# Making the low part of every fourth weight block with an accumulating transfer instead of VectorE

## The chip, the cores and the metric

The kernel runs on one core of one Trainium2 chip. The metric is the device time of one execution in microseconds (us). The kernel before was run three times: 849.24 us median, 848.19 to 850.91.

A core has four compute engines that run at the same time and wait for each other with semaphores: TensorE (PE) multiplies matrices into PSUM, VectorE (DVE) does elementwise work with one or two inputs, ScalarE (ACT) applies a function to one input, GpSimd (POOL) does elementwise work and issues transfers of its own. SyncE (SP) issues transfers only. Sixteen DMA engines carry all transfers.

## The reference

Two layers of a decoder trunk on 256 tokens of width 1024. The stream is normalised and goes through one wide input projection; its columns feed three token mixers (a state-space scan, sliding-window attention with sinks, and forgetting attention), each with a SiLU gate. Each mixer's result is projected back to 1024 columns, the three are merged with sigmoid gates computed from the input, and one output projection is added to the stream:

```python
for layer in range(DEPTH):
    h = rms_norm(x, norm_w[layer])
    proj = jnp.einsum('bsd,de->bse', h, w_in[layer])
    ...
    branch = jnp.einsum('bsiw,iwd->bsid', ys, w_proj[layer])
    g = jax.nn.sigmoid(gates.reshape(b, s, N_BRANCH, d) + gate_bias[layer])
    merged = jnp.sum(g * branch, axis=2)
    x = x + jnp.einsum('bsd,de->bse', merged, w_out[layer])
return rms_norm(x, final_norm_w)
```

All in float32. Nearly all arithmetic is in the products with `w_in` (1024 x 12832), `w_proj` (three of 1024 x 1024) and `w_out` (1024 x 1024).

## The kernel before

**Split products.** TensorE is fed the type fp32r, to which a float32 number is rounded, and the kernel keeps accuracy by splitting both factors: a weight w is hi + lo, hi being w rounded to fp32r and lo the remainder w - hi, and the same for the activations. A product is three matmuls for each 128 rows of the contraction: high with high, low activation with high weight, high activation with low weight (`dense`, L278). So a unit asks for the hi of a weight first, and for the lo two matmuls later.

**Weight parts.** The weights come in pieces of 256 or 512 columns. A piece is cut along the contraction into parts of 128 x 1024 numbers (512 KB): two parts for 256 columns, four for 512. `stream` lists all parts of both layers in the order of use, 266 entries; two of them are narrow pieces of 32 columns that go another way. For a part `load_to` (L332) issues the load into a `raw` buffer on SP's queue (L341), `new_part` (L346) takes a `hi` and a `lo` buffer, and `split` (L261) fills them: ScalarE copies raw to hi (L264), VectorE subtracts hi from raw into lo (L265). There are six buffers each of raw, hi and lo. A part's raw is free again when its lo has been made, and only then can SP load the part six places later; SP's queue is in order. A part's hi and lo are free when PE has used them for the last time.

**How far ahead.** `feed` (L363) emits splits while fewer than AHEAD = 4 parts are held, and whenever PE's program needs a part that isn't there yet. `release` (L377) counts a part off when the last unit that uses it is through with it. A piece is used twice, by a unit for each half of the tokens or of the columns: first pass over all its parts, then a second pass, in which the parts are released one by one. `limit` (L372) stops the splits before the output projection and emits the next few with their place fixed (`pin`, shown as L259), so that they don't get in the way of the merge; that holds for parts 127 to 130 and 260 to 263.

**Order of the work.** PE's order is written out by hand: a list of units (`ops`), between which `pump` puts the small matmuls of the mixers (attention, scan, norms) as generators with delays in estimated PE time. The order of VectorE, ScalarE and GpSimd is made by the language's scheduler, except in the start phase and for pinned instructions. GpSimd does little: the sums of the rotary embedding (L492, L513), the causal selects on the bias of the forgetting attention (L867), powers for the norms (L226, L808) and one add of the merge (L936). Its only transfer is the rotary table at the start (L190).

**The stages.** A layer goes from keys and queries of the sliding window (pieces of 256 and 512) through its gates, convolution inputs, values and the first gate and projection pieces, then the forgetting attention's keys, queries and gates (256 each), then two runs of 512-wide gate and projection pieces (about 318 to 404 us in the first layer and 731 to 817 us in the second), then the output projection.

Of the kernel before, what the change touches and what calls it, by code (L numbers as in the profile page):

```python
# [11 lines left out]
F32 = mybir.dt.float32  # L12
F32R = mybir.dt.float32r
AF = mybir.ActivationFunctionType
ALU = mybir.AluOpType
# [13 lines left out]
T_PP, T_SSD, T_BIAS = 1, 1, 1  # L29
N_RAW, N_SPLIT = 6, 6  # L30
AHEAD = 4
WARM = 30
VERBOSE = False

# [9 lines left out]
def hybrid_trunk(  # L44
# [5 lines left out]
    nc = tc.nc  # L50
# [11 lines left out]
    def T(tag, shape, dtype=F32, bufs=None):  # L62
        count[0] += 1
        return sb.tile(shape, dtype, tag=tag, name=f"{tag}_{count[0]}",
                       bufs=bufs if bufs is not None else BUFS.get(tag, 1))
# [8 lines left out]
    def pmx():  # L74
        return PS("mx", 5)

    act = nc.scalar.activation
# [20 lines left out]
    def transpose(o, a, i):  # L98
        clock["t"] += 0.109
        nc.tensor.transpose(o, a, i)  # L100
# [160 lines left out]
    def split(hi, lo, src, scale=None, keep=lambda f: f):  # L261

        if scale is None:
            keep(act)(hi, src, AF.Copy)  # L264
            keep(tt)(lo, src, hi.bitcast(F32), op=ALU.subtract)  # L265
        else:
            keep(act)(hi, src, AF.Copy, scale=scale)
            keep(stt)(lo, src, scale, hi.bitcast(F32), op0=ALU.mult, op1=ALU.subtract)
# [46 lines left out]
    subs = []  # L315
    ops = []
    stream = []
    state = {"load": 0, "split": 0, "held": 0, "limit": None, "pin": False}
# [13 lines left out]
    def load_to(j):  # L332

        while state["load"] < min(j, len(stream)):
            i, k = stream[state["load"]]
            src, n = subs[i]
            kper = min(NK, 1024 // n)
            raw = T("raw" if n > 32 else "L1", [P, kper, n])
            for c, ap in src:
                m = ap.shape[-1]  # L340
                nc.sync.dma_start(raw[:, :, c:c + m],  # L341
                                  ap.rearrange("(k p) c -> p k c", p=P)[:, k:k + kper, :])
            raws[state["load"]] = raw
            state["load"] += 1

    def new_part():  # L346

        j = state["split"]
        i, _ = stream[j]
        n = subs[i][1]  # L350
        w = pieces.setdefault(i, Piece(n))
        load_to(j + 1)
        if n == 32:
            w.both = T("L2", [P, NK, 2 * n], F32R)
            hi, lo = w.both[:, :, 0:n], w.both[:, :, n:2 * n]
        else:
            hi, lo = T("hi", [P, w.kper, n], F32R), T("lo", [P, w.kper, n], F32R)
            state["held"] += 1
        w.parts.append((hi, lo))
        state["split"] += 1  # L360
        return raws.pop(j), hi, lo

    def feed(i=-1):  # L363

        lim = state["limit"]
        while state["split"] < len(stream) and state["split"] != lim and (
                state["held"] < AHEAD or stream[state["split"]][0] <= i):
            raw, hi, lo = new_part()
            split(hi, lo, raw, keep=pin if state["pin"] else lambda f: f)
            load_to(state["split"] + N_RAW)  # L370

    def limit(j, keep):  # L372

        state["limit"], state["pin"] = j, keep
        feed()

    def release(w, n):  # L377
        if w.n > 32 and n > w.released:
            state["held"] -= n - w.released
            w.released = n  # L380
            feed()

    def run_op(i, f, last):
        if i is None:
            f()
            return
        feed(i)
        w = pieces[i]
        w.last = last
        f(w)  # L390
        if last:
            release(w, NK // w.kper)
# [746 lines left out]
    with tc.manual_schedule(engines={ENG.PE, ENG.DVE, ENG.Activation, ENG.Pool}):  # L1139
        load_to(N_RAW)  # L1140
        warm = pmx()
        for i in range(WARM):
            transpose(warm[:, 0:P], ident, ident)
# [78 lines left out]
```

## Time and profile before

| | before |
|---|---|
| median of three runs | 849.24 us (848.19 to 850.91) |
| the profiled execution: span | 846.0 us (its time outside the span isn't recorded) |
| PE busy | 833.7 us, 99% |
| VectorE busy | 642.3 us, 76% |
| ScalarE busy | 511.6 us, 60% |
| GpSimd busy | 105.7 us, 12% |
| HBM read | 155.22 MB, 186 GB/s over the span |
| TensorE clock granted | 0.996 |

The span runs from the first instruction to the last. "L265 DVE lo<-raw,hi" is a group of instructions: line, engine, what it writes and reads by the program's names, then shapes, count, busy time in us, mean ns of one, and the engine's idle time just before with what ended it. "PEld" is TensorE's weight load, "SPq" the sequencer that issues transfers. Matmuls are pipelined, so a PE row's duration overlaps its neighbours; the distance of their starts is what one costs.

### The profile page before, as it was taken

The page shows a single profiled execution, that of the slowest core. Times are in us where ns is not written, and L with a number is a line of the kernel's source. Part 1 is how long each engine was busy: PE and PEld are TensorE (multiplying, and loading weights), DVE is VectorE, ACT ScalarE, POOL GpSimd, SP SyncE. Part 2 cuts the span into 40 slices and gives each one's busy share as a digit, 9 for nine tenths or more (in the row PEclk, how much of TensorE's full clock was granted, in tenths as well). Part 3 has the DMA queues.
Part 4 walks back from the last instruction along what each step waited for, and adds up shares of the span by engine and source line. Part 5 has one row for each costly group of instructions (what it writes and reads, how often), then busy time and mean ns, then how long its engine had stood idle before and what let it go on. Part 6 is the DMA issues. An engine that isn't in the chain of part 4 may idle for free.

```text
span 846.0 us, 15985 instructions
## 1 busy us (share of the span) xinstructions
PE 833.7 (99%) x5964; PEld 763.4 (90%) x5964; DVE 642.3 (76%) x1403; ACT 511.6 (60%) x1004; POOL 105.7 (12%) x134
## 2 busy tenths in 40 slices
PE   8999999999999999999999999999999999999996
PEld 7989898998999998888989998899899999988896
DVE  5777997998776669656788879879968567785665
ACT  6466777665666667435555667776557667654442
POOL 6410100000140010210014001000003110121000
PEclk9999999999999999999999999999999999999999
DMA  9576565666465545748676465465755654576632
GB/s 303 160 226 197 180 199 163 197 212 184 143 188 177 181 145 189 230 147 292 206 237 218 144 204 157 145 200 182 239 172 176 174 175 152 161 236 211 212 100 76
DMA packets 126638, 158.43 MB, mean 187 GB/s; under 512 B 12784, under 2 KB 88224, under 8 KB 126560
## 3 DMA queue, kind: packets, MB, share of 16 engines
q1 hardware_dynamic: 109456, 140.79, 52.5%
q10 hardware_dynamic: 17056, 16.49, 6.3%
q8 instruction: 47, 0.77, 0.4%
q14 instruction: 31, 0.25, 0.1%
q0 software_dynamic: 48, 0.13, 0.0%
HBM read 155.22 MB, written 2.16 MB: 186 GB/s over the span
## 4 chain that ended last, share of the span: by engine, by line
PE 95%; DMA 3%; DVE 1%; ACT 0%; POOL 0%; issue 0%; SPq 0%; POOLq 0%; DVEq 0%
PE mm L96 82%; PE mx L96 9%; PE mx L100 4%; DMA raw<-in_w_in_dram 3%; DVE lo L265 0%; POOL lo L1154 0%; ACT hi L1153 0%; DVE L L470 0%; ACT L L1013 0%; DVE L L265 0%; ACT L L264 0%; POOLq L1218 0%; ACT L L215 0%; DVE L L996 0%; DVE L L1001 0%
## 5 line engine op out<-in xcount | busy, mean ns | idle before, releaser
L265 DVE TENSOR_TENSOR lo<-raw,hi 128x1024 fp32r<-128x1024 f32 x252 | 308.3, 1235 | 93.8 <-ACT hi L264 84.6
L96 PE MATMUL mm<-hi,L 128*128 128x512 f32 (+1 forms) x1344 | 373.9, 364 | 2.0 <-ACT hi L1153 1.5
L264 ACT ACTIVATE hi<-raw 128x1024 fp32r<-128x1024 f32 x252 | 263.4, 1056 | 93.5 <-PE mm L96 75.5
L96 PE MATMUL mm<-L,hi 128*128 128x256 f32 x1792 | 317.7, 278 | 0.7 <-DVE L L473 0.7
L96 PEld LDWEIGHTS mm<-L,hi 128*128 128x128 f32 x1792 | 277.7, 192 | 7.6 <-issue 3.3
L96 PEld LDWEIGHTS mm<-hi,L 128*128 128x128 f32 x1344 | 241.5, 190 | 32.5 <-issue 2.7
L96 PE MATMUL mm<-L,lo 128*128 128x256 f32 x896 | 246.4, 275 | 0.0
L96 PE MATMUL mm<-lo,L 128*128 128x512 f32 (+1 forms) x672 | 241.4, 361 | 0.6 <-POOL lo L1154 0.6
L96 PEld LDWEIGHTS mm<-L,lo 128*128 128x128 f32 x896 | 171.9, 192 | 0.2
L96 PEld LDWEIGHTS mm<-lo,L 128*128 128x128 f32 x672 | 127.3, 190 | 15.4 <-POOL lo L1154 0.8
L867 POOL TENSOR_SCALAR_AFFINE_SELECT bias<-bias 128x128 f32<-128x128 f32 x64 | 35.9, 597 | 407.5 <-DVE L L736 268.6
L561 ACT ACTIVATE pp<-pp,nm 128x128 f32<-128x128 f32 (+1 forms) x128 | 56.5, 443 | 13.5 <-DVE nm L555 13.5
L698 DVE SCALAR_TENSOR_TENSOR L<-L,vec,L 128x255 f32<-128x255 f32 (+2 forms) x96 | 46.3, 482 | 4.7 <-ACT L L695 3.4
L96 PE MATMUL mx<-L,L 128*64 128x128 f32 (+1 forms) x384 | 34.4, 314 | 0.0
L891 ACT ACTIVATE L<-L 128x512 f32<-128x512 f32 x24 | 15.1, 631 | 29.9 <-DVE L L890 29.7
L573 DVE TENSOR_SCALAR pp<-pp,rsum 128x128 f32<-128x128 f32 (+1 forms) x128 | 32.2, 316 | 0.5
L701 ACT ACTIVATE L<-L 128x256 f32<-128x256 f32 x32 | 13.3, 417 | 31.5 <-DVE L L698 25.9
L96 PEld LDWEIGHTS mx<-L,L 128*64 128x64 f32 x384 | 23.0, 136 | 9.4 <-ACT pp L561 1.3
L782 ACT ACTIVATE L<-mm 128x256 f32<-128x256 f32 x48 | 18.1, 378 | 20.8 <-PE mm L96 20.8
L590 ACT ACTIVATE L<-mx 128x512 f32<-128x512 f32 x48 | 27.0, 597 | 2.7 <-PE mx L100 2.5
L100 PE MATMUL mx<-ident,pp 128*128 128x128 f32 x192 | 26.3, 273 | 0.0
L555 DVE CUSTOM_DVE_ANT_0 pp<-mx,wmask,nsink 128x128 f32<-128x128 f32 x64 | 23.4, 412 | 1.5 <-PE mx L96 1.5
(173 smaller groups left out, 717.5 us busy)
## 6 DMA issues: line engine op xcount, KB each, us to landing
raw<-in_w_in_dram SPq DMA_DIRECT2D x200, 512.0 KB, 4.5
raw<-in_w_proj_dram SPq DMA_DIRECT2D x48, 512.0 KB, 5.5
raw<-in_w_out_dram SPq DMA_DIRECT2D x16, 512.0 KB, 4.6
L<-cumd ACTq DMA_DIRECT2D x8, 512.0 KB, 5.0
bias<-cumd ACTq DMA_DIRECT2D x16, 256.0 KB, 4.0
L<-in_gate_bias_dram ACTq DMA_DIRECT2D x12, 256.0 KB, 3.9
L<-in_x_dram SPq DMA_DIRECT2D x2, 512.0 KB, 4.9
nwb<-in_norm_w_dram SPq DMA_DIRECT2D x1, 512.0 KB, 5.3
```

The costliest lines, as they stand in the source:

```text
L96: nc.tensor.matmul(o, a, b, **kw)
L100: nc.tensor.transpose(o, a, i)
L264: keep(act)(hi, src, AF.Copy)
L265: keep(tt)(lo, src, hi.bitcast(F32), op=ALU.subtract)
L555: nc.vector.tensor_tensor_reduce(out=pp[:, i, sl], in0=score(p, i, b), in1=biases(p, i, b), scale=-0.125, scalar=1.0e30 if ns is None else ...
L561: act(pp[:, i, sl], pp[:, i, sl], AF.Exp, scale=-1.0, bias=nm[:, e:e + 1], accum_out=sums[:, e:e + 1])
L573: ts(pp[:, i, sl], pp[:, i, sl], rs[:, 2 * i + b:2 * i + b + 1], 0.5, op0=ALU.mult, op1=ALU.mult)
L590: act(pT, pt, AF.Copy)
L698: stt(a[:, s:S], x_[:, 0:S - s], y.vec[:, 16 * j + u:16 * j + u + 1], a[:, s:S], op0=ALU.mult, op1=ALU.add)
L782: act(halves(th), p, AF.Tanh, scale=0.5)
L867: nc.gpsimd.affine_select(out=bias[:, i, dst], in_=bias[:, i, src], compare_op=ALU.is_ge, fill=NEG, base=0, pattern=[[-1, P]], channel_mul ...
L891: act(g, g, AF.Tanh, scale=0.5)
```

## The change

From stream index 16 on, every fourth part that is wider than 32 columns and not pinned gets its low part in another way. ScalarE writes hi as before, then ScalarE writes the negative of hi into lo, then GpSimd issues a transfer that adds raw to what stands in lo. The result is the same remainder, raw - hi. The other three parts of four are split as before.

```diff
+SUM_FROM, SUM_EACH = 16, 4
...
+            j = state["split"]
             raw, hi, lo = new_part()
-            split(hi, lo, raw, keep=pin if state["pin"] else lambda f: f)
+            if j >= SUM_FROM and j % SUM_EACH == 0 and subs[stream[j][0]][1] > 32 and not state["pin"]:
+                act(hi, raw, AF.Copy)
+                act(lo, hi.bitcast(F32), AF.Copy, scale=-1.0)
+                nc.gpsimd.dma_start(lo, raw, accum_op=ALU.add)
+            else:
+                split(hi, lo, raw, keep=pin if state["pin"] else lambda f: f)
             load_to(state["split"] + N_RAW)
```

## The prediction, made before the result was known

> **What bounds the kernel now.** I read the page's head first: the busy time of each engine, the chain that ended last, and the two groups that make the high and the low part.
>
> ```profile
> span 846.0 us, 15985 instructions
> ...
> PE 833.7 (99%) x5964; PEld 763.4 (90%) x5964; DVE 642.3 (76%) x1403; ACT 511.6 (60%) x1004; POOL 105.7 (12%) x134
> ...
> PE 95%; DMA 3%; DVE 1%; ACT 0%; POOL 0%; issue 0%; SPq 0%; POOLq 0%; DVEq 0%
> ...
> L265 DVE TENSOR_TENSOR lo<-raw,hi 128x1024 fp32r<-128x1024 f32 x252 | 308.3, 1235 | 93.8 <-ACT hi L264 84.6
> ...
> L264 ACT ACTIVATE hi<-raw 128x1024 fp32r<-128x1024 f32 x252 | 263.4, 1056 | 93.5 <-PE mm L96 75.5
> ```
>
> PE is busy for 833.7 of 846.0 us and makes 95% of the last chain. All that PE does not use is 12.3 us. The last column of the L264 row says that ScalarE, when it stands still, mostly waits for PE to give a hi buffer back: the producers wait for PE, not PE for them. The waits of PE itself confirm it, all seven of them:
>
> ```profile
> PE mm L96 <- ACT hi L1153: 1.5, 1, 1.5
> PE mx L100 <- POOL ident masks.py:199: 1.5, 1, 1.5
> PE mm L96 <- DVE L L473: 0.7, 1, 0.7
> PE mm L96 <- POOL lo L1154: 0.6, 1, 0.6
> PE mx L100 <- DVE L L1165: 0.5, 1, 0.5
> PE mm L96 <- ACT L L264: 0.2, 1, 0.2
> PE mm L96 <- DVE L L265: 0.2, 1, 0.2
> ```
>
> Not one wait for a low part after the start (L1154 is the first four parts). So VectorE time can't be sold for PE time here. What decides is whether a low part that comes later still comes before PE asks for it.
>
> **The edit counted.** Stream index j runs over 266 parts. From 16 to 264 in fours there are 63; 128 and 260 are made while the pin is on (L259's eight parts are 127 to 130 and 260 to 263), none of the rest is 32 wide. So 61 parts change. VectorE loses 61 x 1.235 = 75 us, worth at most what PE waits for VectorE: 0.7 + 0.5 + 0.2 = 1.4 us. ScalarE gains 61 x 1.056 = 64 us (60% to 68% of the span), GpSimd 61 issues, the DMA engines 61 transfers of 512 KB that read two streams and write one.
>
> **How early a low part is now.** The lo matmuls are in program order, eight for each pass of a unit (L278), and the hi activations are in stream order, so the n-th part's hi start and its first lo matmul can be paired by counting:
>
> ```profile
> L96 PE MATMUL mm<-L,lo x896: 275/275/275, 50.4 to 731.0; 128*128 128x256 f32 x180
> ...
> L96 PE MATMUL mm<-lo,L x672: 274/379/541, 12.0 to 838.8; 128*128 128x512 f32 x136, 128*128 128x256 f32 x32
> ...
> L264 ACT ACTIVATE hi<-raw x252: 1037/1057/1076, 19.0 to 825.6; 128x1024 fp32r<-128x1024 f32 x126
> ```
>
> One piece as a picture, parts 105 to 108 of a 512-wide projection: ScalarE makes parts 107 and 108 back to back, and the pass asks for a lo every 0.65 us, two for each part, the seventh at 355.01.
>
> ```profile
> 346.98 2.21 ACT L264 ACTIVATE hi<-raw 128x1024 fp32r<-128x1024 f32 x2
> ...
> 351.13 0.38 PE L96 MATMUL mm<-lo,L 128*128 128x512 f32 x1
> ...
> 355.01 0.38 PE L96 MATMUL mm<-lo,L 128*128 128x512 f32 x1
> ```
>
> Part 108, which changes, starts its hi at 346.98 + 2.21 - 1.06 = 348.1, and PE wants its lo at 355.0: a lead D of 6.9 us. Now it needs 2.3 of them. Paired so for all 61, D runs from part 264 to part 148:
>
> ```profile
> 824.66 2.00 ACT L264 ACTIVATE hi<-raw 128x1024 fp32r<-128x1024 f32 x2
> ...
> 828.63 0.28 PE L96 MATMUL mm<-lo,L 128*128 128x256 f32 x1
> ...
> 454.98 1.06 ACT L264 ACTIVATE hi<-raw 128x1024 fp32r<-128x1024 f32 x1 [0.23 <-PE mm L96]
> ...
> 473.07 0.28 PE L96 MATMUL mm<-L,lo 128*128 128x256 f32 x1
> ```
>
> The first pair is 4.0 us, the second 18.1. In between: 3 parts at 4.0 to 5.2, 8 at 6.7 to 6.9 (all in the 512-wide gate and projection stretches, about 340 to 404 and 750 to 804 us), 8 at 7.3 to 8.8, 12 at 9.3 to 11.1, 16 at 12.0 to 14.7, 14 at 15.4 to 18.1. A lead can't be lengthened by the scheduler: hi is held by its six buffers, which PE frees.
>
> **What a summed low part needs.** Two activations, 2 x 1.06 = 2.1 us, then L: GpSimd's wait and issue, and the transfer to its landing. PE then stalls for max(0, 2.1 + L - D), and since PE is the bound, a stall is a loss in full. No stall shortens the next one: the next summed part's hi buffer is freed by PE after the stall of the one before. Summed over the 61: L = 3: 2 us; 4.1: 5; 4.9: 9; 7.3: 46; 8.1: 64; 9.9: 117; 12: 200; 15: 352.
>
> No row shows an accumulating transfer. The nearest ones:
>
> ```profile
> raw<-in_w_in_dram SPq DMA_DIRECT2D x200, 512.0 KB, 4.5
> ...
> q1 hardware_dynamic: 109456, 140.79, 52.5%
> ...
> DMA to landing us min/median/max: 3.2/4.6/15.0
> ...
> L190 POOL DMA_DIRECT2D rope<-in_rope_dram x1: 926/926/926, 2.7 to 2.7; - x1
> ...
> DMA to landing us min/median/max: 6.3/6.3/6.3
> ...
> L867 POOL TENSOR_SCALAR_AFFINE_SELECT bias<-bias x64: 285/292/6287, 86.5 to 689.2; 128x128 f32<-128x128 f32 x64
> ...
> L867 POOL TENSOR_SCALAR_AFFINE_SELECT bias<-bias 128x128 f32<-128x128 f32 x64 | 35.9, 597 | 407.5 <-DVE L L736 268.6
> ```
>
> A 512 KB weight load lands 4.6 us after issue (3.2 at best). The load queue held each engine for 52.5% of 846 = 444 us for about 268 such loads, so 1.66 us of engine time each; reading a second stream adds about that: 6.2 us. GpSimd's one issue took 0.93 us, in the empty start. Its affine selects take 0.29 us undisturbed and 0.60 on average (35.9 us for 64), so I double the issue to 1.9. L = 6.2 + 1.9 = **8.1 us**, which gives **+64 us**: 17 from the three shortest leads, 27 from the eight at 6.8, 16 from the eight around 8.2, 3 from six at the edge.
>
> Ends: below, the quickest load and the bare issue, 3.2 + 0.93 = 4.1 (+5 us). Above, the rope transfer, the only one that GpSimd issued: 6.3 us for a quarter of the bytes; three quarters more, read twice, add 0.75 x 3.3 = 2.5: 8.8. With one GpSimd op held as long as the longest affine select, 6.3 - 0.3 = 6 us: 14.8 (+343). That hold is visible:
>
> ```profile
> 230.46 8.01 POOL L867 TENSOR_SCALAR_AFFINE_SELECT bias<-bias 128x128 f32<-128x128 f32 x8 [134.89 <-DVE L L736]
> ...
> 231.37 2.36 DVE L265 TENSOR_TENSOR lo<-raw,hi 128x1024 fp32r<-128x1024 f32 x2
> 233.64 0.69 DVE L743 TENSOR_TENSOR L<-L,L 128x512 f32<-128x512 f32 x1
> 234.24 2.36 DVE L265 TENSOR_TENSOR lo<-raw,hi 128x1024 fp32r<-128x1024 f32 x2
> 236.51 0.41 DVE L785 SCALAR_TENSOR_TENSOR L<-L,mm 128x256 f32<-128x256 f32 x1
> ```
>
> The first of these selects was held for as long as VectorE ran tensor_tensors with both inputs in SBUF, five in a row. Whether an issue is held like that, no row shows; I take it half-way, as said, for such runs get rarer with 61 of them gone. The Trainium skill ("SBUF — State Buffer", Who interferes with whom) says that such tensor_tensors block only GpSimd's reads of SBUF and that writing descriptors, an inference there, needs the other side; its rule agrees with the held select, and by it the issue would stay at 0.93, L at 7.1 and the loss at 42 us.
>
> **What lies beside other work.** The negation delays the next part's hi by 1.06 us on ScalarE; the shortest leads are in parts 127 to 131 and 261 to 265, where only 132 and 264 are summed, and 265 comes behind 264's stall: nothing. Each sum waits at the head of GpSimd's queue for its negation, up to 2.1 us, and the rope sums (L492, L513), selects, powers and merge adds behind it come later; their readers are given 3 to 8 us by the order: nothing, and if one is late, its wait adds a few us. SP's next load now waits for the landing of the sum instead of L265:
>
> ```profile
> SPq L341 <- DVE lo L265: 413.0, 163, 10.7
> ...
> 329.72 2.36 DVE L265 TENSOR_TENSOR lo<-raw,hi 128x1024 fp32r<-128x1024 f32 x2 [0.26 <-ACT hi L264]
> ...
> 340.38 1.06 ACT L264 ACTIVATE hi<-raw 128x1024 fp32r<-128x1024 f32 x1 [0.25 <-PE mm L96]
> ```
>
> Those SP waits cost nothing today. The tightest case: the raw of part 100 is free at 329.72 + 1.2 = 330.9, and part 106, loaded into it, is wanted at 340.4, 9.4 us for a 4.6 us load. With L = 8.1 raw is free 7.9 us later, while PE's own stall for part 100 (D = 8.2, so 2.0 us) moves the need too: the load is about 1 us late there, but the next ten such cases have 9.6 to 12 us, and a hi has some us of lead over its matmul. Nothing for the forecast; from L about 10 it would add. The DMA engines carry 61 x 3.3 = 201 us more each, 24% of the span, on top of the load queue's 52.5%.
>
> **Sum.** 846.0 + 64 = 910 us of span. The profiled execution has no time of its own beside its span; the median of the three runs is 849.24 - 846.0 = 3.2 us longer (start and end around the span), which I keep: **913 us**.
>
> **Rivals.**
> *The cover holds* (not slower): a landing in so few us that only parts 264 and 132 are late. It decides at L = 3.2 us, where the loss is 2.5 us, 0.3%, about what a measurement of this kernel can tell from no change; price at L = 3: 2 us, 851. For it: 42 of 61 leads exceed 9 us. Against: the quickest of 268 loads took 3.2 alone, without a second stream or GpSimd's issue. 6%.
> *A short transfer*: nothing contends, L = 3.2 + 0.93 = 4.1 to 4.9, 855 to 858. For: the source is SBUF and not HBM, and loads pause while SP waits. 11%. The Trainium skill ("DMA: Bandwidth & Descriptors", Anatomy of one DMA — SWDGE (gpsimd) path) fits 2.0 us + bytes/436e3 per plain GpSimd DMA, estimated 3.2 us for 512 KB; the rope transfer, 6.3 us for 128 KB, speaks against it.
> *A slow sum*: the engines add at a fraction of the copy rate, or issues are held like the select: L 10 to 15, and raws late on top; +120 to +352, 970 to 1200. 17%.
> *GpSimd's order*: sums queued behind selects that wait for their bias. If every second sum lost 5 us, L = 13.1 for 30 of them: half of 250 and half of 64, +157, 1006. For: its idle time before L867 is 407 us. Against: the sums are emitted parts ahead. 8%.
> *VectorE's relief counts* (faster): at most the 1.4 us above plus some of the start, and never 2.5 by these rows; 3%, for a reordering that I can't see.
>
> **The numbers.** The forecast, L from 4.9 to 9.9, 858 to 966 us, has 55%. Range 855 to 1050: it leaves out 9 in 100 below, and about half of the slow sums above, with a tail of the order case. Faster 0.03, same 0.06, slower 0.91.
>
> **What would show it.** L265 with 191 instead of 252; a new ScalarE group lo<-hi x61 at 1.06; 61 GpSimd issues and their landing time, which with the issue's wait is L: 8 us right, under 5 or over 10 wrong. New waits of PE for the sum's DMA, 60 us in some 24 places, most of 3 us in the 512-wide stretches, and none in the z, k and q parts. PE's busy time unchanged. Waits of ScalarE's hi for the DMA of raw would mean the load chain counts after all; waits of PE for L513, L867 or L936's readers, GpSimd's order. A time under 855 would say that a sum lands like a plain load, over 970 that the engines or GpSimd hold it.

## The result, and the profile after

The changed kernel takes 917.98 us (917.4 to 918.53, four runs) against 848.8 us for the kernel before on the same chip: a ratio of 1.0815, 95% interval 1.0793 to 1.0838, 69 us slower. The forecast was 913 us. The sum is close; the terms under it are not, and the experiments say which. Times are medians of all runs of a kernel; profiles are of one run.

The head of the page of the changed kernel, the chain that ended last, the groups that are new or changed, and the transfers:

```profile
span 916.8 us, 16104 instructions
...
PE 857.4 (94%) x5964; PEld 775.2 (85%) x5964; DVE 578.0 (63%) x1342; ACT 566.4 (62%) x1065; POOL 144.5 (16%) x195
...
q0 software_dynamic: 8832, 32.12, 19.0%
...
PE 70%; DMA 15%; issue 10%; ACT 3%; DVE 1%; POOL 0%; SPq 0%; POOLq 0%; ACTq 0%; DVEq 0%
...
L266 DVE TENSOR_TENSOR lo<-raw,hi 128x1024 fp32r<-128x1024 f32 x191 | 235.7, 1244 | 123.4 <-ACT hi L265 119.5
...
L374 POOL DMA_DIRECT2D lo<-raw x61 | 53.1, 870 | 570.1 <-ACT lo L373 383.0
...
L373 ACT ACTIVATE lo<-hi 128x1024 fp32r<-128x1024 f32 x61 | 64.4, 1056 | 1.2
```

Line numbers are one higher than before, from L365 on seven. The edit does what it says: 61 sums, VectorE's low parts 252 to 191, 61 negations of 1.06 us. PE fell from 99% to 94% of the span and from 95% to 70% of the last chain; 15% is now transfers. PE's waits, and then the mean granted clock of the core:

```profile
PE mm L97 <- DMA lo<-raw: 46.9, 18, 7.5
```

```profile
core 0: 916.8 us, clock 0.970
```

The first row is new: 18 waits for a sum, 46.9 us. The second has no counterpart in the forecast: before, the clock was 0.996. The loss splits into two terms by PE's own time. PE's idle time went from 846.0 - 833.7 = 12.3 to 916.8 - 857.4 = 59.4 us, 47.1 more; PE's busy time, with the same 5964 matmuls, went from 833.7 to 857.4, 23.7 more; 47.1 + 23.7 = 70.8 = 916.8 - 846.0. Most of the second term is the clock. The trace has 55.5 us at half clock (6.9 before), and PE worked in 42.6 of them (3.4 before). At half clock a low product comes every 1.28 us (558.20 and 559.48) in place of 0.65, so this costs (42.6 - 3.4)/2 = 20 us. What makes the other 4 us of busy time stays open. The mean clock alone, 0.030 x 916.8 - 0.004 x 846.0 = 24 us, says too much, for it also counts half clock during which PE stood idle. So two thirds of the loss are stalls and more than a quarter is PE at half speed behind them. Two stretches of the changed kernel show that, each a stall and what follows it (length, busy time of PE, PEld, DVE, ACT and POOL, then PEclk, DMA share, GB/s):

```profile
92.00:100.00 8.00, 4.95 (x26) 4.06 (x24) 6.39 (x11) 6.19 (x12) 2.20 (x5) 1.00 0.69 152
100.00:107.00 7.00, 6.53 (x24) 4.60 (x25) 2.85 (x17) 3.05 (x13) 0.00 (x0) 0.51 0.60 214
389.00:397.00 8.00, 5.78 (x27) 4.72 (x25) 2.25 (x3) 2.01 (x2) 0.90 (x1) 1.00 0.41 128
397.00:407.00 10.00, 4.75 (x11) 3.86 (x12) 2.60 (x3) 2.09 (x3) 0.00 (x0) 0.50 0.99 331
407.00:414.00 7.00, 7.00 (x35) 6.08 (x35) 4.17 (x5) 5.05 (x6) 0.87 (x1) 0.98 0.57 151
```

PE is idle for 3 us by 100, then runs at 0.51 for 7; it is idle from 395 to 402 and has 0.50 from 397 to 407, of which it worked 4.75. The Trainium skill ("TensorE: Matmul & The Clock Gate", Part 1: The HAM clock gate) says that the clock falls to half after an idle window of about 3.4 us and comes back after about as long a busy one; here stalls of 2.0 us and more were mostly enough (one of 2.5 us was not), and the half-clock stretches last 3.4 us, 6.8 or 10.2.

The longest stall is at part 116. Its issue, and PE's first matmul with its low part:

```profile
391.31 0.90 POOL L374 DMA_DIRECT2D lo<-raw  x1 [4.50 <-ACT lo L373]
```

```profile
402.25 0.80 PE L97 MATMUL mm<-lo,L 128*128 128x512 f32 x1 [7.46 <-DMA lo<-raw]
```

GpSimd issues it at 391.3, and PE gets it at 402.2, 10.9 us later. The landing of all 61 is 4.5 us at best, 5.4 in the middle, 10.9 at worst:

```profile
L374 POOL DMA_DIRECT2D lo<-raw x61: 828/862/919, 49.5 to 892.1; - x61
...
DMA to landing us min/median/max: 4.5/5.4/10.9
```

### The profile page after: what moved, and what is told of

The parts are those of the page before. It is cut to its first block, busy times and chain, and to the rows that moved or that the text cites. A ratio compares the mean times of both kernels' runs of the same rounds, so it can differ in the third digit from the quotient of the medians.

```text
span 916.8 us, 16104 instructions
## 1 busy us (share of the span) xinstructions
PE 857.4 (94%) x5964; PEld 775.2 (85%) x5964; DVE 578.0 (63%) x1342; ACT 566.4 (62%) x1065; POOL 144.5 (16%) x195
## 4 chain that ended last, share of the span: by engine, by line
PE 70%; DMA 15%; issue 10%; ACT 3%; DVE 1%; POOL 0%; SPq 0%; POOLq 0%; ACTq 0%; DVEq 0%
PE mm L97 59%; DMA lo<-raw 11%; PE mx L97 8%; PE mx L101 4%; DMA raw<-in_w_in_dram 3%; ACT hi L372 1%; ACT lo L373 1%; DMA L<-cumd 0%; DMA cumd<-L 0%; ACT hi L260 0%; DVE L L705 0%; DVE lo L266 0%; ACT L L216 0%; POOL L L943 0%; DVE pp L580 0%
## 5 line engine op out<-in xcount | busy, mean ns | idle before, releaser
L97 PE MATMUL mm<-hi,L 128*128 128x512 f32 (+1 forms) x1344 | 387.1, 375 | 2.0 <-ACT hi L1160 1.5
L266 DVE TENSOR_TENSOR lo<-raw,hi 128x1024 fp32r<-128x1024 f32 x191 | 235.7, 1244 | 123.4 <-ACT hi L265 119.5
L97 PE MATMUL mm<-lo,L 128*128 128x512 f32 (+1 forms) x672 | 251.7, 376 | 47.2 <-DMA lo<-raw 46.9
L97 PEld LDWEIGHTS mm<-hi,L 128*128 128x128 f32 x1344 | 250.9, 198 | 34.6 <-issue 3.0
L97 PEld LDWEIGHTS mm<-lo,L 128*128 128x128 f32 x672 | 132.6, 198 | 71.4 <-DMA lo<-raw 55.5
L374 POOL DMA_DIRECT2D lo<-raw x61 | 53.1, 870 | 570.1 <-ACT lo L373 383.0
L373 ACT ACTIVATE lo<-hi 128x1024 fp32r<-128x1024 f32 x61 | 64.4, 1056 | 1.2
L568 ACT ACTIVATE pp<-pp,nm 128x128 f32<-128x128 f32 (+1 forms) x128 | 56.8, 445 | 12.8 <-DVE nm L562 11.8
L897 DVE TENSOR_TENSOR L<-mm,L 128x512 f32<-128x512 f32 x24 | 16.5, 688 | 32.0 <-PE mm L97 32.0
L874 POOL TENSOR_SCALAR_AFFINE_SELECT bias<-bias 128x128 f32<-128x128 f32 x64 | 27.0, 471 | 54.6 <-DMA bias<-cumd 53.6
```

The costliest lines, as they stand in the source:

```text
L97: nc.tensor.matmul(o, a, b, **kw)
L373: act(lo, hi.bitcast(F32), AF.Copy, scale=-1.0)
L374: nc.gpsimd.dma_start(lo, raw, accum_op=ALU.add)
L568: act(pp[:, i, sl], pp[:, i, sl], AF.Exp, scale=-1.0, bias=nm[:, e:e + 1], accum_out=sums[:, e:e + 1])
L874: nc.gpsimd.affine_select(out=bias[:, i, dst], in_=bias[:, i, src], compare_op=ALU.is_ge, fill=NEG, base=0, pattern=[[-1, P]], channel_mul ...
```

## Experiments

Theory at the start: a sum costs only where its low part lands later than its lead, and then the stall and the slow clock behind it. Rival: every sum costs, through the DMA engines, ScalarE's negations or GpSimd's queue. All runs are beside runs of the kernel before on the same chip.

| run | us | ratio to before, 95% interval |
|---|---|---|
| changed kernel | 917.98 | 1.0793 to 1.0838 |
| e1_phase2 | 879.17 | 1.0362 to 1.0393 |
| e2_narrow | 847.41 | 0.9973 to 0.9998 |
| e3_negadd | 855.36 | 1.0076 to 1.0110 |
| e4_side | 858.23 | 1.0118 to 1.0153 |
| e4b_side_rows | 849.90 | 1.0002 to 1.0033 |
| e5_fill | 905.98 | 1.0663 to 1.0737 |
| e7_plain | 885.41 | 1.0414 to 1.0464 |
| e8_negfirst | 904.95 | 1.0651 to 1.0683 |
| e9_rows | 909.17 | 1.0681 to 1.0780 |
| e9_before_rows | 846.09 | 0.9971 to 0.9991 |
| e10_all | 866.32 | 1.0180 to 1.0245 |
| e12_narrow_rows | 845.88 | 0.9964 to 0.9985 |

**Other parts, the same number of sums (e1_phase2).**

```diff
-            if j >= SUM_FROM and j % SUM_EACH == 0 and ...
+            if j >= SUM_FROM and j % SUM_EACH == 2 and ...
```

> The summed parts are those with stream index 2 modulo 4 instead of 0: 60 sums, the same work on ScalarE, GpSimd and the DMA engines, but in the 512-wide stretches they fall on the first two parts of a piece, whose hi starts 10 us or more before PE wants the lo; only 4 of 60 leads are under 8 us. Theory (a loss is a low part that comes after its lead, plus the slow clock that follows a stall): 850 to 860 us, with at most one short half-clock stretch after the start. Rival (the loss goes with the number of sums: load on the DMA engines, ScalarE's 64 us, GpSimd's queue): 905 to 920 us.

It lost 32 us and not 69: position alone is worth more than half, and the rival's 905 to 920 is out. But 850 to 860 is missed too. One stall of 11.9 us, with the slow clock behind it, is nearly half of the 32. These are e1's longest stall and the stretch before it:

```profile
391.33 0.80 PE L97 MATMUL mm<-lo,L 128*128 128x512 f32 x1 [11.91 <-DMA lo<-raw]
```

```profile
377.51 0.90 POOL L374 DMA_DIRECT2D lo<-raw  x1 [3.77 <-ACT lo L373]
```

```profile
373.00:383.00 10.00, 3.63 (x8) 2.14 (x8) 5.92 (x6) 8.66 (x10) 1.65 (x2) 0.82 0.05 2
```

The sum was issued at 377.5, and a weight load at 376.5. In the ten microseconds from 373 the DMA engines were busy 5% and moved 2 GB/s. What ran in them, in queue 10, were small constants of the next layer, from 375 on the `d_skip` transfers alone, which `layer_consts` cuts into 4-byte pieces for 64 partitions each. The trace has no packet of a weight load from 373 to 383 and none of a sum before 385, so this sum took 13.8 us to land, where 6.1 is the middle of this run. The rest of the stall is a late issue: ScalarE had stood still for 15.3 us until 374.1, while its queue went through the issues of the same constants. In the changed kernel the same gap stands ahead of part 116 (DMA share 0.05 from 384 to 390).

**Only where leads are long (e2_narrow).**

```diff
-            if ... and subs[stream[j][0]][1] > 32 and not state["pin"]:
+            if ... and subs[stream[j][0]][1] == 256 and j not in (132, 264) and not state["pin"]:
```

> Sums only in the 29 of the 61 parts that are 256 columns wide and have leads of 9 us and more (132 and 264 left to VectorE). Theory (the loss sits where leads are short): no stall on a sum, 849 to 854 us. Rival (each sum costs its share, 69 us times 29 of 61): 875 to 885 us.

847.41 us, the kernel before's time: 29 sums cost nothing, and no wait of PE for a sum is left. With the whole change at 69 us, the loss belongs to the other 32 sums; no run had those 32 alone. Its PE waits, all of them:

```profile
PE mx L101 <- DVE L L1172: 1.5, 1, 1.5
PE mx L101 <- POOL ident masks.py:199: 1.5, 1, 1.5
PE mm L97 <- ACT hi L1160: 1.3, 1, 1.3
PE mx L101 <- DVE L L947: 1.1, 1, 1.1
PE mm L97 <- ACT L L265: 0.3, 1, 0.3
PE mm L97 <- DVE L L266: 0.2, 1, 0.2
```

**The negation without the transfer (e3_negadd).**

```diff
-                nc.gpsimd.dma_start(lo, raw, accum_op=ALU.add)
+                tt(lo, raw, lo.bitcast(F32), op=ALU.add)
```

> The same 61 parts, the same negation on ScalarE, but VectorE adds raw to it instead of a transfer. Theory (the transfer's landing is what comes late): the low part is later than before by one activation, 1.1 us, less than the leads leave: 848 to 852 us. Rival (ScalarE's 64 us more hold up the hi parts or the mixers): 860 us or more.

855.36 us: neither forecast held exactly; 8 us are lost, and no stall reaches 2 us. VectorE's own waits show a price that the transfer doesn't have:

```profile
DVE lo L374 <- ACT lo L373: 52.5, 35, 4.3
```

VectorE's queue is in order, so it stood 52.5 us for negations, with the mixers' work behind it; PE's new waits, most of them 0.9 to 1.8 us, are for mixers' results. So the negation's 64 us on ScalarE is not what costs 69.

**The transfer without the wait (e4_side, e4b_side_rows).**

```diff
-                act(hi, raw, AF.Copy)
-                act(lo, hi.bitcast(F32), AF.Copy, scale=-1.0)
-                nc.gpsimd.dma_start(lo, raw, accum_op=ALU.add)
+                split(hi, lo, raw)
+                nc.gpsimd.dma_start(raw, raw, accum_op=ALU.add)
```

> All parts are split by VectorE as before; for the same 61 parts GpSimd then adds raw onto raw itself by a transfer of the same size, whose result nobody reads, so the 61 transfers and the later release of raw stay and PE waits for none of them. Theory: PE loses nothing but perhaps a late load, 848 to 855 us. Rival (the transfers crowd the weight loads, or raw held some 5 us longer starves the split): 865 to 918 us, with waits of ScalarE for the landing of raw.

858.23 us, between the two. PE waited twice for a hi, 2.6 us at 374 and 2.5 us at 394. The first hi was late because ScalarE's queue was going through the issues of the next layer's constants: ScalarE was idle for 13.5 us before it. The second was late because its raw was late. In e4_side, these two:

```profile
373.04 2.95 ACT L265 ACTIVATE hi<-raw 128x1024 fp32r<-128x1024 f32 x3 [13.54 <-issue]
...
392.56 1.06 ACT L265 ACTIVATE hi<-raw 128x1024 fp32r<-128x1024 f32 x1 [4.59 <-DMA raw<-in_w_in_dram]
```

The second is again at the place of the small pieces. The same with them gone:

```diff
-        y.dsk = T("dsk", [P, NK], bufs=2)
-        for half in range(2):
-            src = d_skip[l:l + 1, :].rearrange("o (j two) -> two o j", two=2)[half]
-            pdma(y.dsk[64 * half:64 * half + 64, :], src.to_broadcast([64, NK]))
+        y.hd = T("hd", [P, 16])
+        pdma(y.hd, d_skip[l:l + 1, :].to_broadcast([P, 16]))
...
+            pin(ts)(y.dsk[hp, :], y.hd[hp, :].rearrange("p (j two) -> p two j", two=2)[:, half, :], 1.0, None, op0=ALU.mult)
```

> VectorE splits every part, 61 transfers add raw onto itself unread, and d_skip is loaded as rows. Theory (the 11 us that the unread transfers cost came where late raws met the gap of the small transfers, 371 to 397 us): 846 to 851 us. Rival (the transfers crowd the weight loads everywhere): 855 to 860 us.

849.90 us, interval 1.0002 to 1.0033: 61 adding transfers that nobody waits for cost this kernel 2 us, or 4 us against the kernel before with the same rows (846.09, e9_before_rows below). One stall for a hi is left, 2.2 us at 372, again behind the issues of ScalarE's constants.

**The stalls filled (e5_fill).**

```diff
+FILL = {28: 17, 56: 12, 100: 11, 108: 9, 112: 12, 116: 35, 124: 3, 132: 56, ..., 264: 34}
...
+            if after is None and i % 3 == 2:
+                for _ in range(fills.pop(w.j0 + k // w.kper, 0)):
+                    nc.tensor.matmul(pt[0:64], zero, bh(k), start=False, stop=False)
             mm(pt, a(k), b(k), start=(i == 0), stop=(i == len(seq) - 1))
```

> The changed kernel with matmuls by a stationary of zeros (they add nothing) put on PE ahead of the first low product of the 19 parts at which it stalled, as many as fit into each stall, 268 in all. Theory (24 us of the loss are half-speed stretches of the clock that follow PE's stalls): the stalls are filled, the clock stays at 1.0 between start and end, 892 to 900 us. Rival (the clock falls for another reason, or the 24 us are waiting in another form): 915 to 925 us.

905.98 us. The clock nearly did what was forecast, the time only half of it. The clock of e5, and part 116's stall filled:

```profile
core 0: 909.3 us, clock 0.993
```

```profile
395.68 7.72 PE L291 MATMUL mm<-hi,zero 128*64 128x512 f32 x35
403.33 0.48 PE L98 MATMUL mm<-lo,L 128*128 128x512 f32 x1
```

The trace has 12.8 us at half clock in place of 55.5, and PE worked in 9.7 of them in place of 42.6: 16 of the 20 us come back when PE isn't idle, with the same sums, the same transfers and the same order. The two slow stretches that are left between start and end stand behind the two longest stalls left, 2.0 and 2.1 us. So the slow clock follows from the idle time. Not all of it reached the time: the fills (48.8 us) and PE's idle time (909.3 - 887.4 = 21.9) together are 70.7 us, 11 more than the 59.4 idle before. A stall's length isn't known ahead to the microsecond, and a fill is fixed.

**A transfer of the same size that doesn't add (e7_plain).**

```diff
-                nc.gpsimd.dma_start(lo, raw, accum_op=ALU.add)
+                nc.gpsimd.dma_start(lo.bitcast(F32), raw)
```

> The changed kernel with a plain transfer of raw into lo where it adds, so the low part is raw itself and the addition is left out. Theory (the second stream that an adding transfer reads costs about 1.2 us of each engine and so of each landing): landing near 4.2 us in place of 5.4, 895 to 908 us. Rival (the landing is fixed cost and queueing): 914 to 920 us.

885.41 us, better than both forecasts. The queue of these transfers and their landing:

```profile
q0 software_dynamic: 8832, 32.12, 9.0%
...
lo<-raw POOLq DMA_DIRECT2D x61, 512.0 KB, 3.6
```

9.0% of 884.2 us for 61 is 1.30 us of each engine; with the addition it was 19.0% of 916.8, 2.86 us. So adding costs 1.55 us of engine time and 5.4 - 3.6 = 1.8 us of landing (0.3 of them in GpSimd's issue), and without it the kernel is 32 us faster. Even so it is 38 us slower than the kernel before, with landings of up to 11.4 us.

**The negative first (e8_negfirst).**

```diff
-                act(hi, raw, AF.Copy)
-                act(lo, hi.bitcast(F32), AF.Copy, scale=-1.0)
+                act(lo, raw, AF.Copy, scale=-1.0)
                 nc.gpsimd.dma_start(lo, raw, accum_op=ALU.add)
+                act(hi, raw, AF.Copy)
```

> The 61 parts as in the change, but ScalarE writes the negative straight from raw into lo first and hi second, so the transfer can be issued one activation, 1.06 us, earlier. Theory (the chain of two activations, issue and landing against the lead sets each stall): some 18 stalls shrink by about 1 us and several half-speed stretches after them go: 885 to 903 us. Rival (a sum lands when the loads queued ahead of it are through, whatever its issue): 912 to 920 us.

904.95 us, just outside the 885 to 903 but 13 us under the change. PE waited 38.5 us for sums in place of 46.9, with a clock of 0.979.

**The small pieces away (e9_rows, e9_before_rows).** The edit on `d_skip` above, on the changed kernel and on the kernel before.

> The changed kernel, with the d_skip constants loaded as one row of 16 numbers to every partition and picked apart on VectorE, in place of two transfers of 4-byte pieces per layer. In the changed kernel these ran from 373 to 396 us, with no packet of the weight loads or of a sum beside them for 6 to 9 us, and the longest stall of PE, 7.5 us, ended behind them. Theory: that stall and its 10 us of half clock shrink, 903 to 909 us. Rival (the sum was late for another reason): 915 to 920 us.

> The kernel before with the same loading of d_skip. Theory: its six raw buffers cover the gap of the small transfers, PE never waits there: 846 to 849 us, no change. Rival (the small transfers cost the kernel before too): 840 to 844 us.

909.17 us (906.36 to 916.58) and 846.09. (The changed kernel's gap begins at about 383; 373 is where it begins in e1_phase2.) The gap in the changed kernel, and the same place in e9_rows:

```profile
384.00:390.00 6.00, 5.84 (x27) 5.15 (x28) 4.09 (x4) 4.63 (x7) 2.79 (x1) 1.00 0.05 0
```

```profile
383.00:389.00 6.00, 6.00 (x30) 5.25 (x29) 3.00 (x4) 4.00 (x5) 0.90 (x1) 1.00 1.03 268
```

Part 116 now stalls 1.4 us in place of 7.5. The kernel before has the gap too (DMA share 0.04 from 367 to 376), but there PE was busy all the while, out of the parts that lay ready; it gains 1.9 us (0.9971 to 0.9991).

**Together (e10_all)**: the sums at 2 modulo 4, the negative first, `d_skip` in rows.

> Sums at stream index 2 modulo 4, the negative written first and straight from raw, and d_skip loaded as rows: the three things by which single runs lost less, together. Theory (leads, the chain of activations and the gap of the small transfers explain the loss): the 32 us of the run with only the position changed lose their longest stall (11.9 us with 17 us of half clock) and 1 us of each other stall: 850 to 858 us. Rival (the sums cost by their number after all): 865 us or more.

866.32 us, a miss in the direction of the rival. Seven waits for sums remain, 13.3 us, and half clock. The longest stands again beside the next layer's constants. Stretches of e10:

```profile
362.00:368.00 6.00, 6.00 (x29) 5.25 (x29) 0.00 (x0) 0.00 (x0) 0.85 (x1) 1.00 0.93 331
368.00:373.00 5.00, 4.70 (x23) 3.77 (x21) 1.85 (x2) 3.60 (x4) 3.12 (x2) 1.00 0.44 129
373.00:379.00 6.00, 0.70 (x3) 0.34 (x2) 4.19 (x4) 5.24 (x7) 1.42 (x2) 0.75 1.00 241
```

```profile
378.66 0.80 PE L97 MATMUL mm<-lo,L 128*128 128x512 f32 x1 [5.30 <-DMA lo<-raw]
```

The DMA share (second from last) is high in the first stretch, so the small pieces are not it; ScalarE (the fourth engine's column) does nothing for 6 us. Its in-order queue goes through nine issues of constants from 358.0 to 369.3, and the hi behind them comes late, with its negative:

```profile
369.40 1.06 ACT L265 ACTIVATE hi<-raw 128x1024 fp32r<-128x1024 f32 x1 [10.36 <-DMA hb<-in_dt_bias_dram]
```

The same place has ScalarE idle for 5.7 us in the kernel before, 13.1 in e4b_side_rows, 13.5 in e4_side and 15.3 in e1_phase2, and in the last three PE then stalled 2.2 to 2.9 us for a hi. That much is read from the rows; no run took these issues off ScalarE.

**The best of what ran (e12_narrow_rows)**: e2_narrow with `d_skip` in rows.

> Sums in the 29 narrow parts with long leads and d_skip loaded as rows: the best of what ran. Theory (VectorE's relief is worth nothing to a kernel that PE bounds, and neither part costs anything): 845 to 848 us, as the kernel before with the rows alone. Rival (28 us less of VectorE brings the mixers' results earlier): 840 to 844 us.

845.88 us, ratio 0.9964 to 0.9985. It is 1.8 us under the kernel before, no more than the rows alone (846.09): VectorE's relief is worth nothing here.

## Why the prediction came out right, step by step

- **The bound and the sign** held. PE bounds the kernel, VectorE's 75 us bought nothing (e2_narrow: 29 sums, no gain; e12 as e9_before_rows), and a late low part costs at least its whole stall.
- **The leads** held in the main. 14 of the 18 stalls, 35 of 47 us, are at parts with a lead under 9 us in the kernel before: 512-wide gate and projection pieces, the two ends of layers, and part 136 of the second layer's 512-wide keys and values. No 256-wide part but 132 and 264 stalled. The other four stalls (parts 28, 56, 160 and 188, 12 us) are at leads of 9.7 to 10.8, where the negation ended 3.6 to 6.1 us after hi began. e2_narrow and e1_phase2 show that leads decide and not number.
- **L = 8.1 us was mis-sized.** Issue waits 0.3 us and the landing, its 0.87 us issue included, is 5.4 in the middle: 5.7. The doubling of GpSimd's issue is wrong (828 to 919 ns for all 61), and 4.6 + 1.66 for the transfer should have been about 4.5, the 5.4 less the issue. By the forecast's own formula a constant 5.7 gives 19 us, not 64.
- **A constant L was wrong as well.** The measured stalls are 47 us. ScalarE put other work between hi and negative in 15 of 61 parts (2.8 to 6.1 us to the end of the negative and not 2.1), which brings the 19 to 24; landings up to 10.9 us account for the rest. With each part's own negation, issue and landing from the trace, and the leads of the kernel before, the formula gives 49 us for the changed kernel (47 measured), 29 for e7_plain (26) and 43 for e9_rows (40). So the formula was right, and one middle value of L was too little to put into it.
- **The term that was missing:** "a stall is a loss in full" is too little. A stall of 2 us or more was mostly followed by half clock: 20 us in all, shown by e5_fill, where 16 of them return. "PE's busy time unchanged" was wrong by 23.7 us.
- So 64 forecast stands for 71 of span measured: 47 of stalls, 20 of clock and 4 unexplained. The stalls were put too high by 17 and the clock left out. That the two errors nearly cancel is luck; with L right and constant, the same sum would have said 868 us. The 3.2 us for start and end are 1.7 in the profiled run (918.53 - 916.8).
- **Rivals.** The cover doesn't hold for the short leads. The short transfer (L 4.1) is what e7_plain comes near, not an adding one, and it lost 38 us and not 5, since single landings took up to 11.4 us. GpSimd's order hardly counts: 57 of 61 sums were issued 0.3 us after their negation, the other four 1.0 to 1.4 us after it. The load on the DMA engines was no danger by itself: in e4b_side_rows they were busy 79% of the span (51.2 + 21.3 + 6.4 + 0.4 + 0.1), and 2 to 4 us were lost.

## What to carry to other kernels

Work moved from a busy engine to a transfer is safe only if its landing, not its engine time, fits into the lead of each place where it is used, and the landing to take is a late one (10.9 us here) and not the middle (5.4). List the leads of all places and look at the shortest: here 29 sums with long leads cost nothing and the other 32 cost all of the 69 us. On a kernel that TensorE bounds, price a stall as its length plus half of the time that TensorE then works at half clock (here 47 + 20 us). And look for transfers in 4-byte pieces before leaning on the DMA queues: here two of 2 KB kept loads and sums from moving for 7 to 10 us.

## What the runs showed that was not expected

- Two transfers of 4-byte pieces, 2 KB each by their size, land in 8.5 to 9.8 us in the kernel before, and while they ran in e1_phase2 the weight load issued at 376.5 moved no packet before 383 and the sum issued at 377.5 none before 385: 2 GB/s in 10 us. As rows of 64 bytes to 128 partitions the same constants landed in 4.8 us with the loads beside them.
- GpSimd's issue of an adding transfer takes 0.86 us, of a plain one 0.53, and VectorE held neither, unlike the affine select that the forecast showed: four of the 61 adding issues lay wholly within a subtraction of L266 and took 828 to 880 ns, the 39 that met none took 849 to 919. The Trainium skill ("SBUF — State Buffer", Who interferes with whom) lets such VectorE work hold only GpSimd instructions that read SBUF; these issues agree.
- Half clock comes in stretches of 3.4 us, one to three after a stall in the changed kernel, and can begin while the stall lasts. After the start, its stalls up to 1.9 us had none; in e3_negadd one of 1.8 us had 3.4 us of it.
